# A hybrid decoder layer on one core: the residual added in PSUM by VectorE, the second triangular solve at two steps a tick, and another entry to the output projection

## The chip, the core and the metric

The kernel runs on one core of one Trainium2 chip. Its engines are TensorE (matrix multiplies into PSUM), VectorE, ScalarE, GpSimd and SyncE (SP), which here only issues transfers. In the profile they are PE (with PEld for its weight loads), DVE, ACT, POOL and SP. The metric is the device time of one execution in microseconds, the median of three runs.

## The reference

One decoder layer in float32 for a sequence of 256 tokens and a model width of 2048. With T = 256, D = 2048, 8 heads of 128 in each branch and a feed-forward width of 5632:

```
h    = rms_norm(x, ln1)
proj = h @ w_in                      # gated-delta q|k|v, beta, decay, z; attention q|k|v; gates A, B
y_a  = gated_deltanet(...) @ w_branch_a      # causal conv 4, chunked delta rule, norm, silu(z)
y_b  = moba_attention(...) @ w_branch_b      # 256 tokens are one block: plain causal attention
x    = x + (sigmoid(gate_a) * y_a + sigmoid(gate_b) * y_b) @ w_out
h    = rms_norm(x, ln2)
u    = causal_dwconv(h @ w_up, ffn_conv, ffn_conv_bias)      # width 3
x    = x + (silu(u_gate) * u_val) @ w_down
out  = rms_norm(x, final_norm)
```

The delta rule needs the inverse of a unit lower triangular matrix for each head and chunk. The kernel takes chunks of 128 tokens, so there are 16 such matrices; it solves them in two units of 8.

## The kernel before, in words

**Products.** Nearly every product is made of three passes over split operands: a float32 weight tile arrives in `wraw`, ScalarE casts it to a rounded high part `wh` (L111), VectorE subtracts to get the low part `wl` (L108), and TensorE adds up high by high, high by low and low by high. `load_w` does that for one load of 128 x 2048 weights, in two pieces of 1024 columns. There are four `wraw` buffers and two each of `wh` and `wl`, so a load can be cast once TensorE is through with the load before the previous one. Weights are fetched on SP's queue.

**Two layouts.** `chunk` puts channels on partitions: two blocks of 128 output channels by 256 tokens into one PSUM tile. `by_token` puts tokens on partitions: two tiles of 128 tokens by 512 channels, and each weight load gives 24 matmuls of 512 columns.

**Ticks.** Side work (the decay, the solves, the attention heads, the transposes of the merged branches) is written as Python generators in the list `bg`. `main_mm` counts the price of the main matmuls (215 for one of 512 columns, 108 for one of 256) and, every 1700, calls `tick`, which resumes each generator once. This is where side work gets its place in program order. A planner then writes each engine's queue from program order as priority and its own estimate of times, so an instruction can run ahead of its place when its engine is free and its inputs are there. `tc.issue_after(ins)` ties instructions behind a given one on their engine.

**A solve** (`gdn_unit`, L541 on) takes 31 steps, each a VectorE product (L564) and a reduction (L565) that depends on the step before it. The first unit yields after every second step, the second after every step. Then a GpSimd transfer writes X to DRAM and another reads it back as `TL` (L568, L570), 12 idle ticks pass, and VectorE turns `TL` in blocks of 32 x 32 (L574), tied behind the latest weight split. Two levels of small products, four more of products with 128 x 128 operands, a square on GpSimd (L635), norms (L637 to L644) and eight output transposes (L652) end it.

**The gates.** The second solve runs beside the gate projection: eight chunks by token, each evicted by two sigmoids (L769) into `gts`. Before the fifth chunk's sigmoids the program resumes the generators until the second solve has ended (L762), closes the solve's buffers, and only then allocates the second `gts` tile. The PSUM pool `ps_mm` has three banks at that time and a chunk takes two.

**Entry of the output projection.** The merged branches are turned to channels by `merged` generators (four transposes, a cast, a split each) into `mc`. The output projection multiplies with `mc`; its first chunk takes its k-steps in an order of its own (`steps`), since the last quarter of `mc` comes late, and resumes all generators at the step `flush`. At this point the PSUM pools are opened anew with wider tiles: three of two banks in `ps_mm`, two of one bank in `ps_sd`.

**Up projection.** 44 chunks of two blocks by channel; each is scaled by the norm (`join`), convolved, gated, and written to `acts`.

**Down projection.** By token, with eight PSUM banks `pd[i][n]` (token half i, 512 channels n) that stay open over all 44 k. For k = 0 each bank is first filled with the residual: four transposes on TensorE of `x1` with an identity (L879); then three matmuls per k and bank. The last four k are taken bank by bank, each bank followed by its share of the final norm and the output.

Of the kernel before, what the change touches and what calls it, by code (L numbers as in the profile page):

```python
# [73 lines left out]
def layer_kernel(ctx: ExitStack, tc: tile.TileContext, xT, pos, cst, ceye, vec, convw, ffw, bdv,  # L74
# [72 lines left out]
    def psum_pools(mm, sd):  # L147
        if pst[2]:
            pst[2].close()
        pst[2] = ExitStack()  # L150
        pst[0] = pst[2].enter_context(tc.tile_pool(name="ps_mm", bufs=mm, space=PSUM, reuse_waits="tile"))
        pst[1] = pst[2].enter_context(tc.tile_pool(name="ps_sd", bufs=sd, space=PSUM, reuse_waits="tile"))

# [61 lines left out]
    def rstd(parts, tp, name):  # L215
        ps = sdt(name)[:, :T]
        mmg(ps, [(ones, t) for t in parts])
        r = tp.tile([P, T], F32, name=name)
        act.activation(r, ps, AF.Sqrt, bias=epst, scale=1.0 / D)
        dve.reciprocal(r, r)  # L220
        return r
# [68 lines left out]
    dve.tensor_tensor(sq[0], sq[0], sq[2], op=ALU.add)  # L290
    dve.tensor_tensor(sq[0][:, 0:2], sq[0][:, 0:2], sq[0][:, 2:4], op=ALU.add)


# [5 lines left out]
    mmg(s, [(wb2[:, k, :], x_[:, k, :]) for k in range(KD) for x_ in (hh, hl)])  # L299
    R1 = rstd([sq[0][:, 0, :], sq[0][:, 1, :]], fk, "R1")  # L300
    R1b = both(R1)
# [237 lines left out]
    def gdn_unit(u):  # L539
# [21 lines left out]
        for r in range(30, -1, -1):  # L561
            tm = gu.tile([P, 8, 32], F32, name="tm", tag="Tm", bufs=1)
            n = 32 - r
            dve.tensor_tensor(tm[:, :, :n], X[:, :, r:], N[:, r:r + 1, r:].to_broadcast([P, 8, n]), op=ALU.mult)  # L564
            dve.tensor_reduce(X[:, :, r], tm[:, :, :n], axis=AX.X, op=ALU.add, negate=True)  # L565
            if r % (2 - u["n"]) == 0:
                yield
# [251 lines left out]
    for c in range(8):  # L819
        if c == 0:  # L820
            steps = ((0, 0, KD - 4), (1, 0, KD - 4), (0, KD - 4, KD), (1, KD - 4, KD))
            ps = chunk(pair(w_o, c), mc, KD, "wo", steps=steps, flush=2)
            y_st.close()
            bkeep = bk.enter_context(tc.tile_pool(name="bkeep", bufs=1, side="right", reuse_waits="tile"))
            x1 = bkeep.tile([P, KD, T], F32, name="x1")
            ffv = bkeep.tile([P, 88, 4], F32, name="ffv")
            sp.dma_start(ffv, ffw)
        else:
            ps = chunk(pair(w_o, c), mc, KD, "wo")
        if c % 2 == 0:  # L830
            s = slice(2 * c, 2 * c + 4)
            sp.dma_start(x1[:, s, :], xT[:, s, :])
        xc = x1[:, 2 * c:2 * c + 2, :]
        for a in (1, 0):
            dve.tensor_tensor(xc, xc, ps[:, :, a, :], op=ALU.add)
        scaled(xc, ln2v, 2 * c, h2[:, :, 0, :], h2[:, :, 1, :])
        if c == 0:
            act.activation(sqa, xc, AF.Square)
        else:
            sq = b.tile([P, 2, T], F32, name="sq2")  # L840
            act.activation(sq, xc, AF.Square)
            if c < 7:
                pool.tensor_tensor(sqa, sqa, sq, op=ALU.add)
    R2 = rstd([t[:, j, :] for t in (sqa, sq) for j in range(2)], bkeep, "R2")
    R2b = both(R2)
# [4 lines left out]
    ak = bk.enter_context(tc.tile_pool(name="ak", bufs=1, side="right", reuse_waits="tile"))  # L850
    acts = ak.tile([P, NF, T], F32, name="acts")
    for c in range(NF):
        ps = chunk([w_up[c], w_up[NF + c]], h2, KD, "up")
        un = b.tile([P, 2, T], F32, name="unf")
        join(un, ps, R2b)
# [9 lines left out]
        pool.tensor_tensor(acts[:, c, :], sg, t[:, 1, :], op=ALU.mult)  # L865
    identb = ak.tile([P, P], F32, name="identb")
    act.dma_start(identb, cst[:, :P])
    fw = ak.tile([P, D], F32, name="fw")
# [5 lines left out]
    pd = [[ps_d.tile([P, 512], F32, name=f"pd{i}_{n}") for n in range(4)] for i in range(2)]  # L874
    order = [(1, 2), (1, 3), (0, 2), (0, 3), (1, 0), (1, 1), (0, 0), (0, 1)]

    def residual(i, n):
        for j in range(4):
            pe.matmul(pd[i][n][:, j * P:(j + 1) * P], x1[:, 4 * n + j, i * P:(i + 1) * P], identb,  # L879
                      start=(j == 0), stop=False, is_transpose=True, skip_group_check=True)  # L880

# [3 lines left out]

    def down(i, n, k, stop=False):
        ah, al, wh, wl_ = wl[k]
        s, c = slice(i * P, (i + 1) * P), slice(n * 512, (n + 1) * 512)
        mmg(pd[i][n], three(ah[:, s], al[:, s], wh[:, c], wl_[:, c]), start=False, stop=stop,
            skip_group_check=True)  # L890

    for k in range(NF):
# [7 lines left out]
        if not last:  # L900
            for i, n in order:
                if k == 0:
                    residual(i, n)
                down(i, n, k)
    for i in range(2):
        sm = b.tile([P, 8], F32, name="sm")
        ots = []
        for n in range(4):
# [3 lines left out]
            act.activation(scr, pd[i][n], AF.Square, accum_out=sm[:, n:n + 1])  # L912
            ots.append(b.tile([P, 512], F32, name="ot_", bufs=5))
            if n < 3:
# [82 lines left out]
```

## Time and profile before

| | us |
|---|---|
| median of 3 runs (1494.28 to 1494.69) | 1494.66 |
| profiled execution | 1494.29 |
| its span, first to last instruction | 1492.5 |
| TensorE busy | 1473.2 |
| VectorE busy | 989.9 |
| ScalarE busy | 728.8 |
| GpSimd busy | 177.2 |

The page gives busy time by engine, then the span in 40 slices, the DMA queues, the chain of waits followed back from the last instruction, and groups of instructions by line. Matmuls are pipelined, and their ends are modelled. The granted clock is a share of TensorE's full speed: 1.00 is 2.4 GHz, 0.50 is 1.2 GHz.

### The profile page before, as it was taken

What the parts mean: (1) busy time and instruction counts of PE and PEld (TensorE: products, weight loads), DVE (VectorE), ACT (ScalarE), POOL (GpSimd) and SP (SyncE); (2) the same over time, 40 slices, a digit from 0 to 9 for tenths busy, and PEclk for the clock granted to TensorE, in tenths of its full rate; (3) what the DMA queues carried; (4) which work ended last, traced back from release to release, by engine and by line L of the source; (5) the groups of instructions that cost most, each with busy time, mean ns of one, the idle gap of its engine ahead of it and who ended that gap; (6) DMA issues with size and microseconds to landing.
All of it is one profiled execution on the core that took longest, in us unless ns stands there. A gap on an engine that the chain in (4) does not pass through costs nothing.

```text
span 1492.5 us, 20716 instructions
## 1 busy us (share of the span) xinstructions
PE 1473.2 (99%) x8383; PEld 1296.7 (87%) x8383; DVE 989.9 (66%) x1397; ACT 728.8 (49%) x969; POOL 177.2 (12%) x135
## 2 busy tenths in 40 slices
PE   9999999999999799999999999999999999999997
PEld 8898899999888688888888888888888888888886
DVE  6997866888844445657766776766767766555554
ACT  5665445554443544435455555555545554444444
POOL 0112000433000400000101111121121110000000
PEclk9999999999999899999999999999999999999999
DMA  9455553544654255556555555555555554555552
GB/s 343 171 189 197 201 184 114 173 159 167 210 194 149 85 210 187 195 210 218 179 218 186 187 192 197 187 184 195 197 175 195 196 187 179 189 190 189 196 196 85
DMA packets 44432, 278.14 MB, mean 186 GB/s; under 512 B 5560, under 2 KB 7664, under 8 KB 12208
## 3 DMA queue, kind: packets, MB, share of 16 engines
q1 hardware_dynamic: 41456, 270.98, 50.7%
q0 software_dynamic: 2016, 3.68, 0.8%
q10 hardware_dynamic: 864, 2.16, 0.4%
q8 instruction: 65, 1.06, 0.3%
q14 instruction: 31, 0.25, 0.0%
HBM read 273.65 MB, written 3.15 MB: 185 GB/s over the span
## 4 chain that ended last, share of the span: by engine, by line
PE 98%; ACT 0%; DMA 0%; DVE 0%; POOL 0%; issue 0%; SPq 0%; DVEq 0%; ACTq 0%; POOLq 0%
PE ps_up L101 33%; PE pd L89 16%; PE ps_gate L101 12%; PE ps_gdn L101 8%; PE ps_moba L101 6%; PE ps_wo L101 6%; PE ps_br L101 6%; PE ps_z L101 3%; PE ps_v L101 3%; PE ps_gdn L257 1%; PE g L89 1%; PE pu L604 0%; PE py L598 0%; DMA xs<-in_xT 0%; PE ps_bd L89 0%; PE po L89 0%
## 5 line engine op out<-in xcount | busy, mean ns | idle before, releaser
L108 DVE TENSOR_TENSOR wl<-wraw,wh 128x1024 fp32r<-128x1024 f32 x496 | 601.3, 1249 | 256.8 <-ACT wh L111 256.6
L111 ACT CAST wh<-wraw 128x1024 fp32r<-128x1024 f32 x496 | 495.3, 1046 | 390.3 <-PE ps_up L101 117.3
L101 PE MATMUL ps_up<-h,wh 128*128 128x512 f32 x1408 | 488.6, 390 | 0.0
L101 PE MATMUL ps_up<-h,wl 128*128 128x256 f32 x1408 | 397.0, 282 | 0.0
L101 PEld LDWEIGHTS ps_up<-h,wh 128*128 128x128 f32 x1408 | 264.2, 188 | 55.4
L101 PEld LDWEIGHTS ps_up<-h,wl 128*128 128x128 f32 x1408 | 266.1, 189 | 0.1
L101 PE MATMUL ps_gate<-wh,hc 128*128 128x512 f32 x512 | 158.4, 395 | 2.8 <-ACT gts L769 2.8
L865 POOL TENSOR_TENSOR acts<-sg,cvf 128x256 f32<-128x256 f32 x44 | 80.8, 1837 | 423.3 <-ACT sg L864 423.3
L89 PE MATMUL pd<-wl,ah 128*128 128x512 f32 x336 | 130.8, 389 | 0.0
L89 PE MATMUL pd<-wh,al 128*128 128x512 f32 x336 | 130.8, 389 | 0.0
L101 PE MATMUL ps_gdn<-hc,wh 128*128 128x256 f32 x704 | 127.1, 281 | 0.0
L101 PEld LDWEIGHTS ps_gate<-wh,hc 128*128 128x128 f32 x512 | 96.7, 190 | 22.9 <-ACT gts L769 3.2
L101 PEld LDWEIGHTS ps_gdn<-hc,wh 128*128 128x128 f32 x704 | 108.3, 188 | 0.4
L859 ACT ACTIVATE cvf<-unf,ffv 128x256 f32<-128x256 f32 x88 | 48.2, 595 | 104.5 <-DVE unf L207 104.5
L101 PE MATMUL ps_gate<-wl,hc 128*128 128x512 f32 x256 | 98.9, 395 | 0.0
L861 DVE SCALAR_TENSOR_TENSOR cvf<-unf,ffv,cvf 128x254 f32<-128x254 f32 (+1 forms) x176 | 77.3, 481 | 32.1 <-ACT cvf L859 31.8
L101 PE MATMUL ps_gdn<-hc,wl 128*128 128x256 f32 x352 | 98.4, 280 | 0.0
L101 PE MATMUL ps_moba<-hc,wh 128*128 128x256 f32 x512 | 92.2, 281 | 0.0
L101 PE MATMUL ps_wo<-mc,wh 128*128 128x512 f32 x256 | 89.0, 390 | 0.4 <-ACT wh L111 0.4
L89 PE MATMUL pd<-wh,ah 128*128 128x512 f32 x336 | 86.7, 391 | 0.0
L111 ACT CAST ah<-acts 128x256 fp32r<-128x256 f32 x44 | 17.9, 406 | 126.0 <-PE pd L89 116.3
L101 PEld LDWEIGHTS ps_moba<-hc,wh 128*128 128x128 f32 x512 | 78.7, 188 | 0.0
(423 smaller groups left out, 1861.6 us busy)
## 6 DMA issues: line engine op xcount, KB each, us to landing
wraw<-in_w_up SPq DMA_DIRECT2D x88, 1024.0 KB, 4.8
wraw<-in_w_dn SPq DMA_DIRECT2D x44, 1024.0 KB, 4.8
wraw<-in_w_gate SPq DMA_DIRECT2D x32, 1024.0 KB, 4.8
wraw<-in_w_gdn SPq DMA_DIRECT2D x22, 1024.0 KB, 4.8
wraw<-in_w_moba SPq DMA_DIRECT2D x16, 1024.0 KB, 4.8
wraw<-in_w_o SPq DMA_DIRECT2D x16, 1024.0 KB, 4.8
wraw<-in_w_z SPq DMA_DIRECT2D x8, 1024.0 KB, 5.4
wraw<-in_w_mv SPq DMA_DIRECT2D x8, 1024.0 KB, 4.8
```

The source lines that it names most:

```text
L89: pe.matmul(ps, a, b, start=(start and i == 0), stop=(stop and i == n - 1), **kw)
L101: pe.matmul(ps, a, b, start=start, stop=stop, skip_group_check=True)
L108: return (eng or dve).tensor_tensor(lo, src, hi.bitcast(F32), op=ALU.subtract)
L111: act.copy(hi, src)
L257: pe.matmul(ps_q0[:, b], r3(wq[b], P)[:, k], xs[:, k], start=(k == b == 0), stop=(k == KD - 1), skip_group_check=True)
L859: act.activation(t[:, j, :], un[:, j, :], AF.Identity, scale=w[:, 2:3], bias=w[:, 3:4])
L861: dve.scalar_tensor_tensor(t[:, j, d:], un[:, j, :T - d], w[:, 2 - d:3 - d], t[:, j, d:], op0=ALU.mult, op1=ALU.add)
L865: pool.tensor_tensor(acts[:, c, :], sg, t[:, 1, :], op=ALU.mult)
```

## The change

- The solve's steps yield after every second step in both units.
- Residual: during the up projection, VectorE turns `x1` in 32 x 32 blocks, a quarter of it at chunks 2, 11, 20 and 29 (`turn`); SP then moves the blocks to their places in `x1`, two transfers of 32 partitions x 8 x 32 floats after each chunk, 64 in all. The 32 transposes with the identity go; the down projection opens its banks with a matmul, and VectorE adds the residual to one bank after that bank's matmuls of one k, from k = 2 to k = 9. The order of the banks is another, and the identity is no longer fetched.
- Output projection: the first chunk's k-steps and the flush are in another order; when the PSUM pools are opened for the second time, `ps_sd` comes first.
- The two norms add two of their partial sums of squares before the matmul with ones: VectorE for the first, GpSimd for the second; each has one matmul less.
- The output tiles are halves of three buffers of 2 x 512 (also used by `turn`) in place of five of 512.

```diff
-        pst[0] = pst[2].enter_context(tc.tile_pool(name="ps_mm", bufs=mm, space=PSUM, reuse_waits="tile"))
-        pst[1] = pst[2].enter_context(tc.tile_pool(name="ps_sd", bufs=sd, space=PSUM, reuse_waits="tile"))
+        for i in ((0, 1), (1, 0))[wide[0]]:
+            pst[i] = pst[2].enter_context(tc.tile_pool(name=("ps_mm", "ps_sd")[i], bufs=(mm, sd)[i], space=PSUM,
+                                                       reuse_waits="tile"))
...
+    dve.tensor_tensor(sq[0][:, 0], sq[0][:, 0], sq[0][:, 1], op=ALU.add)
...
-    R1 = rstd([sq[0][:, 0, :], sq[0][:, 1, :]], fk, "R1")
+    R1 = rstd([sq[0][:, 0, :]], fk, "R1")
...
-            if r % (2 - u["n"]) == 0:
+            if r % 2 == 0:
                 yield
...
-            steps = ((0, 0, KD - 4), (1, 0, KD - 4), (0, KD - 4, KD), (1, KD - 4, KD))
-            ps = chunk(pair(w_o, c), mc, KD, "wo", steps=steps, flush=2)
+            steps = ((0, 0, 8), (0, 8, 12), (1, 0, 4), (0, 12, KD), (1, 4, KD))
+            ps = chunk(pair(w_o, c), mc, KD, "wo", steps=steps, flush=1)
...
+            if c == 6:
+                pool.tensor_tensor(sqa[:, 0], sqa[:, 0], sqa[:, 1], op=ALU.add)
-    R2 = rstd([t[:, j, :] for t in (sqa, sq) for j in range(2)], bkeep, "R2")
+    R2 = rstd([sqa[:, 0, :], sq[:, 0, :], sq[:, 1, :]], bkeep, "R2")
...
+    moves = []
+
+    def turn(q_):
+        blk = r3(x1[:, 4 * q_:4 * q_ + 4, :].rearrange("p k t -> p (k t)"), P)
+        xt = b.tile([P, 8, P], F32, name="xt", tag="ot_", bufs=3)
+        dve.transpose(xt.rearrange("p k t -> p (k t)"), blk.rearrange("p k t -> p (k t)"))
+        for a in range(4):
+            for e in range(4):
+                moves.append((blk[32 * e:32 * e + 32, :, 32 * a:32 * a + 32], xt[32 * a:32 * a + 32, :, 32 * e:32 * e + 32]))
+
     for c in range(NF):
         ps = chunk([w_up[c], w_up[NF + c]], h2, KD, "up")
+        for _ in range(min(2, len(moves))):
+            sp.dma_start(*moves.pop(0))
+        if c in (2, 11, 20, 29):
+            turn(c // 9)
...
-    identb = ak.tile([P, P], F32, name="identb")
-    act.dma_start(identb, cst[:, :P])
...
-    order = [(1, 2), (1, 3), (0, 2), (0, 3), (1, 0), (1, 1), (0, 0), (0, 1)]
+    order = [(0, 0), (0, 1), (1, 0), (1, 1), (1, 2), (1, 3), (0, 2), (0, 3)]
 
     def residual(i, n):
-        for j in range(4):
-            pe.matmul(pd[i][n][:, j * P:(j + 1) * P], x1[:, 4 * n + j, i * P:(i + 1) * P], identb,
-                      start=(j == 0), stop=False, is_transpose=True, skip_group_check=True)
+        p3 = r3(pd[i][n], P)
+        dve.tensor_tensor(p3, p3, x1[:, 4 * n:4 * n + 4, i * P:(i + 1) * P], op=ALU.add)
...
             for i, n in order:
-                if k == 0:
+                down(i, n, k, start=(k == 0))
+                if k == 2 + order.index((i, n)):
                     residual(i, n)
-                down(i, n, k)
...
-            ots.append(b.tile([P, 512], F32, name="ot_", bufs=5))
+            if n % 2 == 0:
+                o2 = b.tile([P, 2, 512], F32, name="ot_", bufs=3)
+            ots.append(o2[:, n % 2, :])
```

## Rows read from the trace of the kernel before

**Rows 1.** The page: busy time by engine, weight casts, and the chain by engine
```profile
PE 1473.2 (99%) x8383; PEld 1296.7 (87%) x8383; DVE 989.9 (66%) x1397; ACT 728.8 (49%) x969; POOL 177.2 (12%) x135
...
PE 98%; ACT 0%; DMA 0%; DVE 0%; POOL 0%; issue 0%; SPq 0%; DVEq 0%; ACTq 0%; POOLq 0%
...
L111 ACT CAST wh<-wraw 128x1024 fp32r<-128x1024 f32 x496 | 495.3, 1046 | 390.3 <-PE ps_up L101 117.3
```

**Rows 2.** Stretches: from:to, length, busy us by engine, granted clock, DMA share, GB/s
```profile
144.00:184.00 40.00, 40.00 (x204) 34.19 (x203) 33.80 (x76) 18.56 (x20) 0.78 (x2) 1.00 0.53 194
240.00:262.00 22.00, 22.00 (x189) 21.86 (x188) 18.94 (x46) 13.90 (x18) 2.84 (x3) 1.00 0.28 97
364.00:497.40 133.40, 133.40 (x663) 112.69 (x661) 76.22 (x119) 54.47 (x68) 6.33 (x6) 1.00 0.51 179
497.40:507.74 10.34, 2.31 (x8) 1.38 (x8) 3.92 (x12) 5.47 (x8) 1.89 (x1) 0.72 0.01 2
507.74:512.00 4.26, 4.26 (x10) 3.39 (x11) 0.00 (x0) 4.26 (x9) 3.14 (x3) 0.50 0.00 0
535.00:555.00 20.00, 20.00 (x90) 16.57 (x89) 7.69 (x8) 8.82 (x10) 0.00 (x0) 1.00 0.55 197
659.70:673.40 13.70, 12.60 (x74) 10.76 (x73) 6.23 (x8) 5.38 (x7) 0.00 (x0) 1.00 0.78 302
757.70:1241.00 483.30, 483.30 (x2790) 428.45 (x2790) 336.37 (x438) 254.72 (x354) 80.09 (x43) 1.00 0.54 191
1255.00:1310.00 55.00, 55.00 (x245) 45.53 (x244) 27.88 (x30) 23.38 (x31) 0.00 (x0) 1.00 0.55 192
```

**Rows 3.** The chain that ended last, 494 to 512: start, us, what
```profile
498.16 1.90 POOL so L635
...
507.00 0.70 ACT gts L769
```

**Rows 4.** Line L560, ahead of each solve: ns, first and last start
```profile
L560 DVE MEMSET N<- x2: 85/85/85, 143.9 to 362.1; 128x32 f32 x2
```

**Rows 5.** VectorE in order of time: start, us, line, operation
```profile
183.02 0.42 DVE L565 TENSOR_REDUCE X<-tm 128x8 f32<-128x256 f32 x1
...
401.90 0.42 DVE L565 TENSOR_REDUCE X<-tm 128x8 f32<-128x256 f32 x1
...
413.75 2.36 DVE L108 TENSOR_TENSOR wl<-wraw,wh 128x1024 fp32r<-128x1024 f32 x2 [3.08 <-ACT wh L111]
...
441.96 2.36 DVE L108 TENSOR_TENSOR wl<-wraw,wh 128x1024 fp32r<-128x1024 f32 x2 [3.56 <-ACT wh L111]
444.25 1.24 DVE L574 STREAM_TRANSPOSE U<-TL 128x1024 f32<-128x1024 f32 x1
```

**Rows 6.** GpSimd in order of time, at the second solve's read back
```profile
405.89 0.90 POOL L570 DMA_DIRECT2D TL<-dT  x1 [2.38 <-DMA dT<-X]
```

**Rows 7.** DMA: a queue (packets, MB, share); issues (count, KB each, us to landing)
```profile
q0 software_dynamic: 2016, 3.68, 0.8%
...
TL<-dT POOLq DMA_DIRECT2D x2, 512.0 KB, 5.8
...
dT<-X POOLq DMA_DIRECT2D x2, 128.0 KB, 3.6
```

**Rows 8.** The chain, 236 to 256: the first solve's last output transposes
```profile
253.98 0.44 PE pot L652 x4
```

**Rows 9.** The chain, 1240 to 1250: the first of eight such groups of transposes
```profile
1240.96 0.44 PE pd L879 x4
```

**Rows 10.** Groups by line: busy us, mean ns, idle before
```profile
L835 DVE TENSOR_TENSOR x<-x,ps_wo 128x512 f32<-128x512 f32 x16 | 11.0, 687 | 15.5 <-PE ps_wo L101 15.2
```

**Rows 11.** VectorE in order of time, at the last up chunk's eviction
```profile
1244.23 0.68 DVE L205 TENSOR_TENSOR unf<-ps_up,unf 128x512 f32<-128x512 f32 x1
```

**Rows 12.** The chain, 33 to 38: the first norm's two matmuls
```profile
36.71 0.86 PE R L89 x4
```

**Rows 13.** GpSimd in order of time, at the second norm's last addition
```profile
743.41 1.48 POOL L843 TENSOR_TENSOR sqa<-sqa,sq 128x512 f32<-128x512 f32 x1 [9.61 <-ACT sq L841]
```

More of the change, by code (lines that the diff above doesn't have):

```diff
@@ L884, in layer_kernel, with down @@
     tail = hp.tile([P, 2, 2, 2048], F32R, name="tail", tag="hc")
-    def down(i, n, k, stop=False):
+    def down(i, n, k, start=False, stop=False):
         ah, al, wh, wl_ = wl[k]
         s, c = slice(i * P, (i + 1) * P), slice(n * 512, (n + 1) * 512)
-        mmg(pd[i][n], three(ah[:, s], al[:, s], wh[:, c], wl_[:, c]), start=False, stop=stop,
+        mmg(pd[i][n], three(ah[:, s], al[:, s], wh[:, c], wl_[:, c]), start=start, stop=stop,
             skip_group_check=True)
```

## The prediction, made before the result was known

> **What bounds the kernel now.** I read the busy table and the chain of waits first: TensorE is busy 1473.2 of 1492.5 us, the next engine 66%, and 98% of the chain that ended last is TensorE's [rows 1]. So an edit pays only where it takes work off TensorE or closes a gap in it; work on VectorE, ScalarE, GpSimd or a DMA queue is free as long as TensorE doesn't wait for it. Second came the table by stage [rows 2]: in the long stages TensorE is busy all the time, and there are two holes, 497.40 to 507.74 (2.31 us busy in 10.34) and 659.70 to 673.40 (12.60 in 13.70). In the row after the first hole the granted clock is 0.50, that is 1.2 GHz, the lower of its two levels; ten matmuls took 4.26 us there, against 20.00 for 90 at 2.4 GHz. Third, the chain inside the first hole [rows 3] and the order on VectorE before it [rows 4, 5].
>
> The profiled execution took 1494.29 us for a span of 1492.5; the 1.8 us around it stay. The median of three is 1494.66. The sum below is worked out on the profiled execution, and its difference is taken off the median.
>
> **The second solve, two steps a tick.** The hole is the end of the second solve. After its last matmul TensorE waits for a square on GpSimd (L635), then a VectorE reduction, a square root, the scaling, eight transposes (L637 to L653), and at last for the first sigmoid of the fifth gate chunk [rows 3]. That sigmoid writes the second `gts` tile, in memory that is only handed over when the solve's buffers are released (L761 to L767); until then the PSUM of that chunk is full and TensorE has no bank for the next one. So the cost of the hole is set by when the solve ends against when the fifth chunk ends.
>
> What the edit changes is not the solve's speed. Both solves start at 143.9 and 362.1 [rows 4] and end their last step at 183.4 and 402.3 [rows 5]: 39.5 us with two steps a tick and 40.2 with one, because VectorE takes a step whenever it is free. What counts is the number of ticks: the steps now yield 16 times instead of 31, so everything behind them (the 12 idle ticks, then the block transpose at L574, which is queued behind the latest weight split) is reached 15 ticks earlier. A tick is 8 matmuls of 512 columns, a weight load 24, so that is 5 loads. On VectorE the block transpose stands right behind the split at 441.96; five loads earlier is the split at 413.75 [rows 5]: 28.2 us. Its input can be there: the read back is issued at 405.89 [rows 6] and such a read lands in 5.8 us [rows 7], 411.7, before the split ends at 416.1. So 4 us of slack are left.
>
> All that follows moves with it: the sigmoid that started at 507.00 could start at 478.8 as far as the solve goes. The tail may stretch, since it will run beside gate work: in the first solve the last output transposes ended at 254.4 [rows 8], in the middle of a stretch where TensorE never idles (22.00 in 22.00 us [rows 2]). TensorE needs the bank at 497.40, so 18 us of stretch are covered. What is late next is nothing of the solve: the fifth chunk's own matmuls.
>
> The worth: 10.34 us of hole, less the eight transposes that TensorE has to do anyway (four take 0.44 [rows 8], so 0.88), is 9.46; and ten matmuls at 0.426 instead of 0.222 us [rows 2] are another 2.0. Together 11.5. The bounds: no gain at all if the solve's end isn't set by the ticks; below nothing if the denser steps put weight splits late. Against a loss stands the first solve, two steps a tick in matmuls of the same shape: TensorE 40.00 busy of 40.00 with VectorE at 33.80 [rows 2]. I take 11.5.
>
> **The residual.** Off TensorE go 32 transposes, in 8 groups of 0.44 us [rows 9]: 3.5. Added are, on VectorE, 4 block transposes at 1.24 [rows 5] and 8 additions in PSUM, priced at 0.69 by the addition of a PSUM and an SBUF operand at L835 [rows 10]; on SP's queue 64 transfers of 32 KB, two a chunk. The block transposes lie in the up projection, where VectorE is busy 336.37 of 483.30 us [rows 2]; 5.0 more go into 147 free. An addition comes after one group of the down projection and before that group's next turn, seven groups or 4.7 us later (a turn of 24 matmuls is 5.3 us by the row 535 to 555 in [rows 2]); VectorE there is busy 27.88 of 55.00 [rows 2], and only one addition falls into each turn. Cover for all: cost nothing. Without cover it is 8 x 0.69 = 5.5 and 4 x 1.24 = 5.0.
>
> The first turn gets tighter: with no transposes between its groups TensorE reaches the bank of the last up chunk after six groups of 0.67 us, 4.0 us instead of 6.6, at about 1245.0 [rows 2, 9], and the eviction that frees it ran from 1244.23 for 0.68 us, to 1244.91 [rows 11]. I take no wait; up to 1 us if the eviction slips behind a weight split (two take 2.36 [rows 5]).
>
> The transfers: no row has one on SP's queue in runs of 128 bytes. From below: GpSimd's queue carried 3.68 MB in packets that took 0.8% of the span, 11.9 us [rows 7]; it holds transfers in such runs, and at its rate the 2.1 MB of the change take 6.8 us spread over 480 [rows 2]. From above: a transfer could hold all engines for as long as the 128 KB one needs to land, 3.6 us [rows 7]. The up projection leaves 46% of each 11.0 us chunk free, 5.05 us [rows 2]. I take the lower row, since it counts packet time and not latency: nothing on the path. A transfer waits on SP for its block transpose, and behind it wait the weight fetches; four weight buffers stand ahead of them, so a microsecond is covered.
>
> The Trainium skill, "VectorE: DVE Perf Modes", section "Rules for kernel authors", says to transpose 128 x 128 on TensorE where a PSUM destination will do, since VectorE only turns 32 x 32 blocks (section "The three transpose paths"). By that rule the change is a bad trade, and in busy time it is: 3.5 us saved for 10.5 of VectorE and 64 transfers. By the rows it is a good one, as only TensorE is short of time. Priced by busy time alone, the residual would cost 7.0 instead of giving 3.5, and the sum would be 1488.3.
>
> **The output projection's entry.** Of 13.70 us TensorE idles 1.10 [rows 2]: once before the first matmul and once before the second chunk, whose weight buffer stays taken until the interleaved steps are nearly through. In the new order block 0 is through 12 of block 1's k-steps earlier, about 4 us, and a cast of 1.05 [rows 1] and a split of 1.2 [rows 5] are what the next chunk needs first: covered. The first wait is for a PSUM bank; the new pool order may close it, leave it, or add up to one eviction (0.69). I take 1.0 of gain, between -0.7 and 1.1.
>
> **The two norms.** Each drops one matmul of the four or two that take 0.86 us a pair [rows 12]: 0.43 each, 0.9 together. The first adds a 256-column VectorE addition under 0.69, ahead of splits; the second a GpSimd addition of half the 1.48 us one that ended at 744.9 [rows 13], 6 us ahead of the matmul that reads it. Both covered.
>
> Sum: 11.5 + 3.5 + 1.0 + 0.9 = 16.9, profiled 1494.29 to 1477.4, and on the median 1477.8.
>
> **Rivals.**
> 1. *The solve ends no earlier, or another wait holds the banks.* For it: the solve ran 40 us with either yield, so its end need not follow ticks; against: the 42 us between its last step and the block transpose have no other owner (the data was there by 411.7). The hole stays: 1494.66 - 5.4 = 1489.3; half of it, 1483.5.
> 2. *VectorE's order becomes the wait.* An addition stands in line behind a split whose own cast waits for TensorE, and TensorE for the addition. For it: splits fill half of VectorE's time there; against: 27 us free in 55 [rows 2]. All eight uncovered: 1483.3. With the four block transposes uncovered as well, so that VectorE's whole addition lands on the path: 1488.3. This last is what the skill's rule comes to.
> 3. *The transfers starve the weights: slower.* Place: the 32 chunks with two transfers each. It decides from (5.05 + 16.9 / 32) / 2 = 2.8 us of the whole stream for each transfer; at 3.6 us each chunk is short by 2.15 us, 69 in all, and the time is 1547. For it: short runs in the same queue as the weights. Against: the packet time of GpSimd's queue, which makes it 0.1 us.
> 4. *A new order written by the planner loses as much as the edits win.* It lays every engine's queue out anew. Within 0.2%, about 3 us, the least that a measurement of this kernel tells from no change: 1492 to 1497.
>
> **Chances.** Forecast (1475.5 to 1480) 0.66; rival 1 0.11, rival 2 0.10 for the additions and 0.03 for all of it, rival 3 0.04, rival 4 0.06 (of it 0.01 slower). Faster by over 0.2% 0.90, within 0.2% 0.05, slower 0.05. The range 1475.5 to 1487.0 takes in the forecast, the additions of rival 2 and half of rival 1; the rest, under 0.2, is left out.
>
> **What would show it.** Right: no stretch from 364 us to the output projection with TensorE under full and no clock of 0.50 there; the block transpose of the second solve near 416; the chain of waits free of GpSimd's square; no L879; the down projection's first turn in 5.4 to 5.6 us; and a span of about 1475.6. Wrong: a hole still standing before the sixth gate chunk (rival 1), TensorE waits released by VectorE at the additions (rival 2), fetches that land late in the up projection with a DMA share near 1 (rival 3).

## The result, and the profile after

The changed kernel takes 1476.73 us (median of four runs, 1475.83 to 1477.89) against 1494.47 for the kernel before on the same chip: a ratio of 0.9882, 95% interval 0.9865 to 0.9899, and 17.7 us less. The forecast was 1477.8. The profiled execution of the changed kernel took 1477.89 us for a span of 1476.1.

The first two rows of the profile after are the busy time by engine and the chain of waits by engine (a q behind an engine's name is its sequencer, which waits and issues):

```profile
PE 1465.6 (99%) x8347; PEld 1291.1 (87%) x8347; DVE 1000.5 (68%) x1410; ACT 727.8 (49%) x969; POOL 177.3 (12%) x136
...
PE 99%; DMA 0%; SPq 0%; DVE 0%; ACT 0%; issue 0%; DVEq 0%; ACTq 0%
```

Against [rows 1], TensorE has 36 instructions and 7.6 us less, VectorE 13 instructions and 10.6 us more, and GpSimd's part of the chain is gone. The rest of the 16.4 us of span is time in which TensorE stood. The stretches of [rows 2], each moved to where the same work now lies (columns: from:to, length, busy us by engine, granted clock, DMA share, GB/s):

```profile
365.30:498.70 133.40, 133.40 (x668) 112.94 (x667) 80.36 (x131) 59.68 (x76) 8.22 (x7) 1.00 0.48 172
498.70:509.04 10.34, 10.34 (x47) 8.37 (x46) 4.99 (x3) 8.16 (x13) 9.52 (x7) 1.00 0.23 90
509.04:513.30 4.26, 4.26 (x20) 3.56 (x19) 4.26 (x3) 2.00 (x2) 4.26 (x3) 1.00 0.61 239
648.00:661.70 13.70, 13.70 (x82) 12.09 (x81) 8.44 (x11) 5.58 (x7) 0.00 (x0) 1.00 0.76 279
745.20:1228.50 483.30, 483.30 (x2789) 428.44 (x2789) 339.04 (x441) 254.62 (x354) 80.12 (x43) 1.00 0.57 196
1242.50:1297.50 55.00, 55.00 (x245) 45.54 (x244) 33.58 (x39) 23.08 (x30) 0.00 (x0) 1.00 0.58 208
```

The first hole is full (10.34 of 10.34), the stretch behind it runs at a granted clock of 1.00 and not 0.50, and the output projection's entry is full as well. The up projection's row differs by 2.7 us of VectorE and three points of DMA share.

Both traces, and those of the experiments, are compared by stages. This table is worked out from the first matmul of each stage (us from it to the first matmul of the next; the last two columns are the down projection up to the last matmul, and from there to the end of the span):

```
                 gates+solve  branches  output proj.  up      down    end
before           204.06       90.92     90.90         489.18  243.55  8.16
after            192.31       89.87     89.89         489.17  240.12  7.71
a1_steps_back    204.10       89.87     89.89         489.17  240.12  7.72
a2_no_idle       194.12       90.91     90.89         489.18  243.55  8.12
a3_fourth_bank   199.67       90.90     90.88         489.18  243.55  8.19
a4_adds_together 192.31       89.88     89.89         489.17  240.12  7.71
b1_old_steps     192.28       89.88     90.82         489.17  240.12  7.70
b2_old_pools     192.31       90.91     89.68         489.17  240.13  7.73
b3_old_residual  192.28       89.88     89.89         489.17  243.55  8.15
c1_five_times    192.34       89.88     89.89         514.80  240.12  7.75
c3 (fw by SP)    192.28       89.87     89.89         501.64  240.12  7.72
c2 (small)       192.28       89.88     89.89         489.17  240.12  7.68
d1_merge         192.28       87.05     90.63         489.95  240.16  7.70
d2_spread        192.30       87.05     90.63         488.54  240.12  7.73
```

A stage that an edit doesn't touch repeats within 0.07 us from run to run, so effects of a tenth of a microsecond can be read here that the times (95% intervals of about 0.3%, 5 us) can't show. What isn't in the table is the part ahead of the gates: it varies by 2 us from execution to execution (the first gate matmul lies at 365.03 to 367.05 in the runs with the new norm, at 365.73 to 366.25 in the three with the old one). TensorE waits there for the first loads, and in two executions its clock falls behind such a wait: in the profiled one of the changed kernel it waits 1.79 us up to 8.59, and the granted clock is 0.72 from 8 to 14 us. That is most of why its work lies 1.3 us later than in the kernel before.

The differences of the first two lines are -11.75, -1.05, -1.01, -0.01, -3.43 and -0.45, together -17.70; the two medians differ by 17.74. That these agree to 0.04 us is chance: the part ahead of the gates, and the first norm with it, is in the medians alone.

### The profile page after: what moved, and what is told of

Read it like the earlier page. It is cut to its first block, busy times and chain, and to the rows that moved or that the text cites. A ratio compares the mean times of both kernels' runs of the same rounds, so it can differ in the third digit from the quotient of the medians.

```text
span 1476.1 us, 20717 instructions
## 1 busy us (share of the span) xinstructions
PE 1465.6 (99%) x8347; PEld 1291.1 (87%) x8347; DVE 1000.5 (68%) x1410; ACT 727.8 (49%) x969; POOL 177.3 (12%) x136
## 3 DMA queue, kind: packets, MB, share of 16 engines
q1 hardware_dynamic: 58864, 273.08, 52.4%
q8 instruction: 65, 1.06, 0.3%
## 4 chain that ended last, share of the span: by engine, by line
PE 99%; DMA 0%; SPq 0%; DVE 0%; ACT 0%; issue 0%; DVEq 0%; ACTq 0%
PE ps_up L101 33%; PE pd L89 16%; PE ps_gate L101 12%; PE ps_gdn L101 8%; PE ps_moba L101 6%; PE ps_wo L101 6%; PE ps_br L101 6%; PE ps_z L101 3%; PE ps_v L101 3%; PE ps_gdn L258 1%; PE g L89 1%; PE pu L606 0%; PE py L600 0%; DMA xs<-in_xT 0%; PE ps_bd L89 0%; PE po L89 0%
## 5 line engine op out<-in xcount | busy, mean ns | idle before, releaser
L108 DVE TENSOR_TENSOR wl<-wraw,wh 128x1024 fp32r<-128x1024 f32 x496 | 602.1, 1250 | 259.0 <-ACT wh L111 258.5
L89 PE MATMUL pd<-wh,ah 128*128 128x512 f32 x336 | 92.2, 389 | 0.0
```

What stands on the lines that cost most here:

```text
L89: pe.matmul(ps, a, b, start=(start and i == 0), stop=(stop and i == n - 1), **kw)
L108: return (eng or dve).tensor_tensor(lo, src, hi.bitcast(F32), op=ALU.subtract)
```

## The experiments

**The solve.** Three runs ask what the hole hangs on. The first takes the changed kernel and puts only the ticks back:

```
-            if r % 2 == 0:
+            if r % (2 - u["n"]) == 0:
                 yield
```

> The changed kernel with the second solve alone put back to one step a tick. Theory (the number of ticks sets when the solve ends, and the hole in TensorE hangs on that end): the block transpose of the second solve goes from 417.3 back to about 445, the hole of 10.3 us behind the fifth gate chunk and the half clock after it return, and the time is 1476.7 + 11.7 = 1488.4 us. Rival (the hole went because the planner laid the queues out anew after the other edits): no hole, 1476.7.

Measured: 1488.15 us (ratio to the kernel before 0.9959, 0.9945 to 0.9973). The stage is back at 204.10, all others are those of the changed kernel. From the chain of waits of that run:

```profile
497.90 1.90 POOL so L637
...
502.32 0.44 PE pot L654
...
506.74 0.70 ACT gts L771
```

It is [rows 3] again. So the whole 11.75 us belong to the ticks, and no other edit has a share in it.

The second takes the kernel before and cuts the second unit's 12 idle ticks behind the read back:

```
         pool.dma_start(TL, dT[:, :P].rearrange("p s c -> s p c"))
-        yield from wait(12)
+        yield from wait(12 * (1 - u["n"]))
```

> The kernel before, steps still one a tick, but the second solve's 12 idle ticks between the read back of TL and the block transpose taken away: 12 ticks are 4 loads, 22.5 us. Theory (only the count of ticks matters, not how densely the steps come): the block transpose moves from 444.2 to about 421.7, and the hole shrinks. How much is left tells how the tail behaves: with the 62.7 us that the tail took in the kernel before, the sigmoid comes at 484.4 and no hole is left, -11.7 (1482.8); with the 80 us that it took in the changed kernel it comes at about 502, some 5 us after TensorE wants the bank, and the gain is only 4 to 7 us (1488 to 1490). Rival (denser steps are what matters): no change, 1494.5.

Measured: 1484.74 us (0.9938, 0.9923 to 0.9953), stage 194.12. Here are the two block transposes of the solves (ns, first and last start):

```profile
L574 DVE STREAM_TRANSPOSE U<-TL x2: 1236/1242/1247, 194.4 to 422.3; 128x1024 f32<-128x1024 f32 x2
```

and TensorE's waits between 495 and 508 us (engine, line, waited for: us, times, longest):

```profile
PE ps_gate L101 <- ACT gts L769: 0.6, 1, 0.6
PE ps_gate L101 <- DVE wl L108: 0.4, 1, 0.4
```

The steps are as sparse as before, and the hole is down to 1.06 us: it is the count of ticks, not how densely the steps come. Neither of the two ways in which the tail might go was right. With the transpose at 422.3 the sigmoid came at 498.7: 76 us, not 63 and not 80.

The third leaves the solve alone and gives TensorE a bank instead:

```
-    psum_pools(3, 5)
+    psum_pools(4, 4)
```

> The kernel before, with four PSUM banks for the main matmuls and four for the side work (before: three and five) up to the output projection. Theory (in the hole TensorE waits for the bank that the fifth gate chunk holds until the late sigmoid): the sixth chunk has its two banks, the solve still ends near 505, and the hole is gone or down to the eight transposes: -9 to -11.7, 1483 to 1485.5 us, if four side banks are enough for the solves. Rival (TensorE stands in its own queue behind the solve's output transposes, whatever banks are free): the first part of the hole, 497.40 to 502.58, stays and only the second, 2.8 us, goes, with some of the half clock: -2.8 to -4, about 1491.

Measured: 1489.49 us (0.9967, 0.9955 to 0.9979), stage 199.67, in between the two. The windows from the place where TensorE used to stop:

```profile
497.40:513.60 16.20, 16.20 (x88) 13.70 (x86) 6.71 (x6) 7.14 (x9) 1.89 (x1) 1.00 0.43 139
513.60:519.33 5.73, 1.75 (x10) 0.96 (x9) 4.80 (x12) 5.36 (x8) 0.00 (x0) 0.86 0.38 160
519.33:524.00 4.67, 4.67 (x11) 3.70 (x12) 0.00 (x0) 4.67 (x10) 2.40 (x2) 0.50 0.65 226
```

and five pieces of its chain of waits (start, us, what), with one of the kernel before behind them:

```profile
494.34 5.70 PE ps_gate L101 x25
...
502.05 3.65 PE ps_gate L101 x16
...
508.00 1.06 ACT wh L111
509.08 3.05 DVE wl L108 x2
...
518.59 0.70 ACT gts L769
```

```profile
491.07 2.76 PE ps_gate L101 x12
```

With a bank free TensorE did go on, 16.2 us further; so it was the bank. But the tail of the solve slid along: its square on GpSimd began at 508.0 and not at 498.2, its sigmoid at 518.6 and not at 507.0, and a hole of 4 us of idle time opened behind the next chunk, with the clock of 0.50 behind it. The chain says why. Of those 11.6 us, 9.9 are lost ahead of the square: the tail was 3.3 us late already at 494.34, and then gate matmuls of 5.70 and 3.65 us stand on TensorE itself between the tail's last products, where the kernel before had 2.76. Behind the square a cast on ScalarE and two splits on VectorE stand ahead of the tail's small instructions, for the other 1.7. In the kernel before, the tail was quick at its end because TensorE had stopped. This is what a wait looks like that gives way when it is relieved: what released it was being helped by the wait.

**The additions.** All eight in one turn:

```
-                if k == 2 + order.index((i, n)):
+                if k == 2:
                     residual(i, n)
```

> The changed kernel with all eight additions of the residual in the third turn of the down projection, in place of one each in turns three to ten. A turn is 5.3 us of TensorE; eight additions are 8 x 0.69 = 5.5 us of VectorE, and a turn's splits another 2.8. Theory of the prediction (an addition is free as long as it finds a gap of VectorE): here it does not, the next weights' split comes late, and TensorE waits 1 to 3 us in all: 1478 to 1480. Rival (weights are split two turns ahead, so that even eight at once are covered): 1476.7.

Measured: 1476.19 us (0.9880, 0.9865 to 0.9895), down projection 240.12. My expectation failed; the rival was right. The additions:

```profile
L896 DVE TENSOR_TENSOR pd<-pd,x x8: 692/692/695, 1240.2 to 1245.5; 128x512 f32<-128x512 f32 x8
```

and the windows up to and around them:

```profile
1226.70:1240.00 13.30, 13.30 (x59) 10.73 (x59) 9.71 (x14) 8.82 (x13) 0.74 (x1) 1.00 0.42 153
1240.00:1246.20 6.20, 6.20 (x29) 5.15 (x28) 6.20 (x11) 2.31 (x3) 0.00 (x0) 1.00 0.91 330
```

VectorE is full for 6.20 us, and TensorE is full beside it. The weight splits around the additions end at 1242.04 and begin again at 1246.47, and no matmul waits: two buffers of split weights stand about one turn of 5.44 us ahead. The additions can be called free here with a margin of all eight.

**The output projection's entry**, one half of the edit undone at a time. First the k-steps:

```
-            steps = ((0, 0, 8), (0, 8, 12), (1, 0, 4), (0, 12, KD), (1, 4, KD))
+            steps = ((0, 0, KD - 4), (1, 0, KD - 4), (0, KD - 4, KD), (1, KD - 4, KD))
...
-            ps = chunk(pair(w_o, c), mc, KD, "wo", steps=steps, flush=1)
+            ps = chunk(pair(w_o, c), mc, KD, "wo", steps=steps, flush=2)
```

> The changed kernel with the old order of the output projection's first chunk (12 k-steps of each block, then 4 of each), the new order of the PSUM pools kept. Theory (two stalls at this entry, each with its own cause: a buffer of split weights for the second, a PSUM bank for the first): the stall before the second chunk comes back with 0.66 us of idle TensorE and some 0.2 us of refilling behind it, the first stays closed: 1476.5 + 0.8 = 1477.3. Rival (the pool order alone closed both): no stall, 1476.5.

Measured: 1477.14 us (0.9886, 0.9869 to 0.9904); the output projection's stage is 90.82, 0.93 longer. Then the pools:

```
-        for i in ((0, 1), (1, 0))[wide[0]]:
+        for i in (0, 1):
...
-    order = [(0, 0), (0, 1), (1, 0), (1, 1), (1, 2), (1, 3), (0, 2), (0, 3)]
+    order = [(1, 2), (1, 3), (0, 2), (0, 3), (1, 0), (1, 1), (0, 0), (0, 1)]
```

> The changed kernel with the old order of the PSUM pools from the output projection on, and the old order of the eight groups in the down projection that goes with it. Theory: the stall of 0.44 us before the first matmul of the output projection comes back, with 0.2 to 0.4 of refilling, and the down projection enters on whatever bank the old order meets first, without a stall: +0.6 to +0.9, 1477.3. Rival (the new steps alone closed both, by moving the planner's order): no stall, 1476.5.

Measured: 1477.68 us (0.9887, 0.9872 to 0.9903); branches and output projection together are 180.59, 0.83 longer. The windows show which stall came back: with the old steps the second one,

```profile
646.00:650.00 4.00, 4.00 (x22) 3.44 (x21) 3.30 (x5) 2.00 (x2) 0.00 (x0) 1.00 0.75 262
658.00:662.00 4.00, 3.33 (x20) 2.68 (x19) 2.85 (x3) 3.90 (x4) 0.00 (x0) 1.00 0.83 330
```

with the old pools the first:

```profile
646.00:650.00 4.00, 3.56 (x20) 2.87 (x19) 3.31 (x5) 2.48 (x3) 0.00 (x0) 1.00 0.69 262
658.00:662.00 4.00, 4.00 (x25) 3.55 (x24) 3.13 (x5) 1.84 (x3) 0.00 (x0) 1.00 1.03 406
```

Each half has its own stall, as the theory had it. And each costs more than its idle time: 0.93 for 0.67 idle, 0.83 for 0.44. The matmuls around the second stall show why:

```profile
659.38 0.39 PE L101 MATMUL ps_wo<-mc,wh 128*128 128x512 f32 x1
660.43 0.39 PE L101 MATMUL ps_wo<-mc,wl 128*128 128x256 f32 x1 [0.67 <-DVE wl L108]
660.65 0.39 PE L101 MATMUL ps_wo<-mc,wh 128*128 128x512 f32 x1
```

A matmul is shown 0.39 us long, but without a stall the next one starts 0.23 us behind it, and a short one's successor 0.12 behind. Here it is 1.05 and 0.22, so 0.82 and 0.10 us more: the overlap of two matmuls is lost as well, and the idle time doesn't count it. The same count gives 0.68 us for the first stall; what makes it 0.83 isn't shown.

**The residual** on TensorE again, with its identity and its five separate output buffers:

```
-        p3 = r3(pd[i][n], P)
-        dve.tensor_tensor(p3, p3, x1[:, 4 * n:4 * n + 4, i * P:(i + 1) * P], op=ALU.add)
+        for j in range(4):
+            pe.matmul(pd[i][n][:, j * P:(j + 1) * P], x1[:, 4 * n + j, i * P:(i + 1) * P], identb,
+                      start=(j == 0), stop=False, is_transpose=True, skip_group_check=True)
```

> The changed kernel with the residual as before: 32 transposes on TensorE in the down projection's first turn, no block transposes, transfers or additions, and the five separate output buffers. Theory: the 8 x 0.44 = 3.5 us on TensorE come back and nothing else in the up and down projections; if the last 0.45 us at the end of the kernel hangs on the paired output buffers, that too: 1476.5 + 3.4 to 3.9 = 1480.2. Rival (the additions or transfers cost something hidden in the 3.44 us that the down projection gained): the down projection changes by more than 3.5 us.

Measured: 1480.49 us (0.9906, 0.9890 to 0.9921). The down projection is back at 243.55 (+3.43), the up projection unchanged, and the end of the span back at 8.15 (+0.44). The transposes stand in the chain as in [rows 9]:

```profile
1230.69 0.70 PE pd L89 x3
1231.39 0.44 PE pd L896 x4
```

**The transfers.** Each one issued four more times, into memory that nothing uses until the end:

```
+    spare = [r3(fw, 256)[32 * a:32 * a + 32, :, 32 * e:32 * e + 32] for e in range(8) for a in range(4)]
...
-            sp.dma_start(*moves.pop(0))
+            dst, src = moves.pop(0)
+            for _ in range(4):
+                spare.append(spare.pop(0))
+                sp.dma_start(spare[-1], src)
+            sp.dma_start(dst, src)
```

> The changed kernel with every transfer of the residual issued four more times into memory that is unused until then: ten a chunk in place of two. Theory (a transfer costs the stream of weights 0.26 us of packet time, as the share of its queue went up by 16.8 us for 64 in the changed kernel): ten are 2.6 us of the 5.05 that a chunk of the up projection leaves free, nothing waits, 1476.5. Rival of the prediction (a transfer holds the stream for as long as the nearest one needs to land, 3.6 us): 36 us in a chunk of 11, some 25 us late in each of 32 chunks, 2280. Anything above 0.5 us each shows as TensorE waiting for weights.

Measured: 1502.49 us (1.0051, 1.0033 to 1.0068): slower than the kernel before. Neither number was near. Three kinds of wait stood in the up projection; here its waits from 1005 to 1024 us and then from 805 to 818:

```profile
ACT wh L111 <- DMA x<-xt: 16.2, 1, 16.2
...
PE ps_up L101 <- ACT wh L111: 11.6, 1, 11.6
...
DVE xt L864 <- DMA x<-xt: 8.4, 1, 8.4
...
PE ps_up L101 <- DVE wl L108: 3.4, 1, 3.4
```

The longest is the experiment's own: the copies land in `fw`, and the fetch of `fw` on ScalarE's queue waited for the last of them with a weight cast behind it. The second is in the change as well: there are three buffers `xt`, so VectorE stands before the fourth block transpose until the first buffer is moved out, with the weight splits queued behind it. The third are eight stalls of 0.1 to 0.8 us. So a second run fetched `fw` on SP's queue, and a third one issued the same number of transfers with an eighth of the data in the extra ones:

```
-                sp.dma_start(spare[-1], src)
+                sp.dma_start(spare[-1][:, :1, :], src[:, :1, :])
```

> The run with every residual transfer issued five times, but with the final norm's weights (whose buffer takes the extra copies) fetched on SP's queue behind the last transfer, so that ScalarE no longer stands 16 us before that fetch. Both theories: the one stall of 11.64 us goes, the many small ones stay: 1502.5 - 11.6 = 1490.9.

> As the run before it, but each of the four extra transfers carries an eighth: 32 rows of 128 bytes in place of 256, the same number of instructions on SP. Theory 1 (what runs out is SP's time: each transfer takes 0.65 us there, ten and two weight fetches 7.7 us, and with its waits a chunk's 11.0 us): the small stalls stay and the time is that of the run before it, about 1491. Theory 2 (what runs out is the stream: the DMA share was 0.80 there against 0.54): the extra bytes fall from four times the residual to half of it, the stalls go, about 1477.

Measured: 1488.06 us (0.9955, 0.9939 to 0.9971) for the first, up projection +12.47, of it 7.7 us idle (the longest, 3.5, is the second kind of wait again); 1476.39 us (0.9880, 0.9863 to 0.9896) for the small ones, up projection unchanged. Windows of 820 to 1000 us with the full copies:

```profile
820.00:900.00 80.00, 80.00 (x464) 70.91 (x463) 54.77 (x73) 41.41 (x58) 13.98 (x8) 1.00 0.79 211
900.00:1000.00 100.00, 96.92 (x550) 84.22 (x549) 65.51 (x84) 48.88 (x67) 13.67 (x8) 1.00 0.79 205
```

with its waits, of SP's queue from 744 to 1020 us and of ScalarE from 945 to 1020:

```profile
SPq L875 <- DMA wraw<-in_w_up: 20.1, 26, 1.6
...
ACT wh L111 <- DMA wraw<-in_w_up: 26.2, 13, 3.6
```

and with the small ones, the second window and SP's wait in the same stretch:

```profile
900.00:1000.00 100.00, 100.00 (x579) 88.67 (x578) 69.29 (x92) 52.22 (x73) 17.00 (x9) 1.00 0.64 211
```

```profile
SPq L875 <- DMA wraw<-in_w_up: 5.6, 19, 0.5
```

In 85 us from 900 on, SP issued 96 full transfers and 13 weight fetches, or 109 small ones and 15 fetches; TensorE needs 15.5 fetches (two a chunk of 11.0). SP got through more instructions in the second case, 75.9 us of issuing against 68.7, so its own time isn't what ran out first. With a DMA share of 0.79 SP's waits grow and the weights come late; at 0.64 they don't. That favours the stream over SP. It isn't a clean separation, since SP has only some 9 us in 85 left even with the small ones.

**Further on the same road.** The changed kernel with two more things taken off TensorE: the second norm's three matmuls become one, and six of the eight groups of transposes of the merged branches become block transposes and transfers:

```
+        if c < 3:
+            gt = r3(g_, P)
+            xg = m.tile([P, 4, P], F32, name="xg", bufs=2)
+            dve.transpose(xg.rearrange("p k t -> p (k t)"), g_)
+            for a in range(4):
+                for e in range(4):
+                    (sp, pool)[e % 2].dma_start(gt[32 * e:32 * e + 32, :, 32 * a:32 * a + 32],
+                                                xg[32 * a:32 * a + 32, :, 32 * e:32 * e + 32])
+            yield from wait(6)
...
-    R2 = rstd([sqa[:, 0, :], sq[:, 0, :], sq[:, 1, :]], bkeep, "R2")
+    dve.tensor_tensor(sq[:, 0], sq[:, 0], sq[:, 1], op=ALU.add)
+    dve.tensor_tensor(sq[:, 0], sq[:, 0], sqa[:, 0], op=ALU.add)
+    R2 = rstd([sq[:, 0, :]], bkeep, "R2")
```

> The changed kernel with its own idea taken to two more places. Six of the eight groups of four transposes that turn the merged branches (pt_m) go to VectorE blocks and 16 transfers each, half on SP's and half on GpSimd's queue, in the branches' stage; and the second norm's three matmuls become one after two more VectorE additions. Theory (TensorE is the only engine that is short): 6 x 0.44 + 2 x 0.43 = 3.5 us less, 1476.5 - 3.5 = 1473.0. Rival (here the result is wanted at once, by the output projection: 96 transfers in 67 us of the stage come on top of its weights): the output projection or the weights wait, and the gain is 0.9 or less, or a loss of some us.

Measured: 1474.55 us (0.9864, 0.9849 to 0.9879). The branches are 2.82 us shorter. Two new stalls take some back: 0.73 before the third quarter of `mc`, and 0.94 at 769 us. The waits around the latter, from 764 to 772 us:

```profile
DVE xt L877 <- DMA x<-xt: 4.9, 1, 4.9
...
PE ps_up L101 <- DVE wl L108: 0.9, 1, 0.9
```

It is the wait for an `xt` buffer again, with weight splits behind it on VectorE. The last run addresses both:

```
-            yield from wait(6)
+            yield from wait((6, 6, 3)[c])
...
-        dve.transpose(xt.rearrange("p k t -> p (k t)"), blk.rearrange("p k t -> p (k t)"))
+        with tc.issue_after(lows[-1].ins):
+            dve.transpose(xt.rearrange("p k t -> p (k t)"), blk.rearrange("p k t -> p (k t)"))
```

> The run before it (d1), with its two new stalls addressed: each of the four block transposes of the residual is tied behind the weight split of its own chunk (3, 12, 21, 30 of the up projection), so that the transfers come 16 at a time and not 64 in 55 us; and the third pair of merged groups is read back after 3 ticks in place of 6, so that its split no longer stands behind the output projection's first weights. Theory (the stall of 0.94 us at 769 came from the bunched transfers, that of 0.73 at 648 from the late split): both go, and 1.9 to 2.2 us with their refilling: 1474.5 - 2.0 = 1472.5. Rival (16 transfers in one chunk still put the next weights late, or the earlier split waits for its transfers on ScalarE): no gain, 1474.5, with stalls in other places.

Measured: 1473.87 us (0.9866, 0.9849 to 0.9883). One of the two went. The stretch with the bunched transfers in d1:

```profile
745.00:800.00 55.00, 54.05 (x311) 47.49 (x310) 41.70 (x56) 30.86 (x43) 7.53 (x4) 1.00 0.80 216
```

the same in d2, where the four block transposes lie at 761 to 1061 us:

```profile
745.00:800.00 55.00, 55.00 (x320) 48.83 (x319) 41.28 (x54) 31.54 (x44) 5.96 (x5) 1.00 0.66 221
```

and the wait that stayed in d2:

```profile
PE ps_wo L101 <- DVE mc L805: 0.7, 1, 0.7
```

From the first gate matmul to the last matmul of all, the changed kernel takes 1101.36 us, d1 1100.07 and d2 1098.64. So d2 is the fastest of the kernels here, by 2.7 us of its trace; the intervals of the times overlap with those of the changed kernel, and by them alone it isn't shown.

## Why the prediction was right, step by step

**The solve (11.5; measured 11.75).** Ticks are the cause (a1, a2), and the block transpose stands where it was put, right behind the split that follows five loads earlier; both started 1.3 us later in this execution:

```profile
415.05 2.36 DVE L108 TENSOR_TENSOR wl<-wraw,wh 128x1024 fp32r<-128x1024 f32 x2 [3.08 <-ACT wh L111]
417.33 1.24 DVE L576 STREAM_TRANSPOSE U<-TL 128x1024 f32<-128x1024 f32 x1
```

The sentence "the sigmoid that started at 507.00 could start at 478.8" was wrong as a picture. ScalarE after:

```profile
495.08 1.26 ACT L655 ACTIVATE ya<-pot,vc 128x512 f32<-128x512 f32 x2
496.36 1.28 ACT L771 ACT_TABLE_LOAD   x1
497.66 1.27 ACT L771 ACTIVATE gts<-ps_gate,cols 128x512 f32<-128x512 f32 x2
```

From block transpose to sigmoid it was 62.8 us before [rows 3, 5] and is 80.3 now. Of the 18 us that I called covered, 17.6 were used, and TensorE wanted the bank at about 498.7 (497.40 and the later start). That looks like a narrow escape. a2 and a3 show that it is not so sharp: the tail's pace is set by the gate's work, matmuls, casts and splits, that it stands among. One load later costs 1.06 us of idle TensorE, five loads cost 8.0. I had priced the tail as if it had a speed of its own.

**The residual (3.5; 3.43).** The removed term was near, and the wait that I had taken as none was there. In the kernel before, the first turn took 9.09 us and a later one 5.44 (not 5.3), so the transposes were worth 3.65. In the changed kernel the first turn takes 5.67, above the 5.4 to 5.6 that I had named, and each of the next forty 5.44. TensorE reaches the bank of the last up chunk after six groups, as forecast, but its eviction had slipped behind two weight splits (1229.46, 2.36 us):

```profile
1231.73 0.68 DVE L206 TENSOR_TENSOR unf<-ps_up,unf 128x512 f32<-128x512 f32 x1
```

The matmul into that bank starts at 1232.47, and 0.23 us come back. That 3.5 was so close owes something to these two misses, which offset each other.

The cover of the other work held, though not as told. The transfers are not "two a chunk": the planner pulled the block transposes forward, and all 64 transfers went out in 55 us:

```profile
L870 SPq DMA_DIRECT2D x<-xt x64: 585/609/1678, 744.7 to 800.2; - x64
```

My lower price of 0.1 us of the stream each was too low. SP's queue before and after (packets, MB, share):

```profile
q1 hardware_dynamic: 41456, 270.98, 50.7%
...
q1 hardware_dynamic: 58864, 273.08, 52.4%
```

The share went from 50.7% to 52.4%, that is from 756.7 to 773.5 us, or 0.26 us each; the 256 extra ones of c1 give 0.26 again (56.0% of 1501.5 us). The upper price, 3.6, was far off, and what each takes of SP, 0.61 us, I had left out. In those 55 us SP issued the 64 transfers and 8 weight fetches where 10 were needed; the four weight buffers covered the two that were missing, and c1 and c3 show what happens when such a stretch goes on. And one wait I hadn't named: VectorE stands before the fourth block transpose until its buffer is moved out, with weight splits queued behind it. That was 1.5 us in the changed kernel and harmless, 4.9 in d1 and 8.4 in c1, where TensorE lost 0.94 and 3.4 us. So of this step the result came out, and of its reasons only "four weight buffers stand ahead of them".

The Trainium skill, "VectorE: DVE Perf Modes", section "Rules for kernel authors", would have had these transposes on TensorE. The trace speaks against it in this kernel: 3.43 us gained (b3). The Trainium skill, "DMA: Bandwidth & Descriptors", section "Rules for kernel authors", says that transfers under 64 KB pay mostly overhead. That agrees: one of 32 KB takes 0.26 us of the stream, and by an estimate its bytes would take 0.09 at the mean rate of SP's queue in the kernel before (270.98 MB in 756.7 us). Of SP it takes 0.61 us, where a weight fetch of 1024 KB takes 0.54 among the transfers and 0.33 (the median) in the up projection as a whole.

**The output projection's entry (1.0; 1.63).** The branches and the output projection lost 2.06 together; 0.43 of it is put down to the norm's matmul, by the first norm's rows, since no run puts the second norm back alone. The term that was mis-sized is the price of a stall: I took the idle time of 1.10, the runs say 0.83 and 0.93 for the two, 0.1 more together than the 1.63 that are left.

**The two norms (0.9).** The second is in the 2.06. The first reads off the chain of waits, where [rows 12] had 0.86:

```profile
38.44 0.43 PE R L89 x2
```

**Not in the sum:** the end of the span, 0.45 us. It is there in all runs with the paired output buffers and in none without (b3: 8.15), so it goes with the residual's part. Up to the last output's issue, 3 us after the last matmul, the two kernels agree to 0.01 us, and its landing comes 6.80 and 6.83 us after that matmul. What makes the part behind the landing shorter is open.

**The rivals.** The first is excluded by a1 and a2, though a3 gave it some right: what is behind the bank would not have stood still. The second is excluded for the additions by a4, and for the block transposes by the up projection's 489.17 against 489.18; in small it stood in the first turn, with 0.23 us. The third is excluded at the price it named, but c3 shows that its mechanism is real. Of the fourth, the table shows no stage that lost.

## What to carry to other kernels

When side work ends a hole, ask what it stands among: work that is quick while the main engine waits gets slow once the wait is gone, so a relieved wait can come back later, in part. Price a stall by what the stage loses when it is put back, not by its idle time alone. And for many small transfers count three things, the issuing queue, the stream, and how far the planner will bunch them, against the loads that are buffered ahead.

## What was not expected of the hardware

A VectorE addition into a PSUM bank whose accumulation stays open took 0.69 us, as an eviction does, and eight in a row left TensorE full at a granted clock of 1.00 (a4). TensorE's clock fell to 0.50, its lower level of 1.2 GHz, in a3 as in the kernel before: in the row behind 5.73 us in which it was busy for 1.75. In a2, where it was idle for 1.06 us in two pieces at that place, the granted clock is 1.00 from 495 to 512 us. In the profiled execution of the changed kernel it is 0.72 from 8 to 14 us, behind a wait of 1.79 us; in d2 it is 1.00 there, behind one of 1.54. A transfer of 4 KB took SP 0.59 us and one of 32 KB in the same run (c2) 0.63, both in runs of 128 bytes, so SP's price hardly depends on the size.
